# Encoder layer on one core: the last gate half turned through DRAM, attention parts of the output projection first, down groups ending on two plain units

## The chip, the cores and the metric

The kernel runs on one core of one Trainium2 chip. The metric is device time in microseconds (us) of one execution; lower is better. Of the kernel before, three runs gave a median of 1146.52 us (1145.9 to 1146.56).

## The reference

One layer of a bidirectional encoder for 256 tokens of 2048 features, all in fp32. With `norm` for RMS normalisation with a gain:

```
u = norm(x) @ w_in                       # 2048 -> 5120: q, k, v (1024 each), xr, yg (1024 each)
attn = neighbourhood_attention(q, k, v)  # 8 heads of 128, 4x64 grid of tokens
rec  = rglru_bidirectional(xr) * gelu(yg)        # conv, two gated scans; 8 blocks of 128
mixed = [norm(attn), norm(rec)] @ w_out  # 2048 -> 2048
h = x + norm(mixed)
f = norm(h)
ff = (silu(f @ w_gate) * (f @ w_up)) @ w_down    # 2048 -> 5632 -> 2048
h = h + norm(ff)
h = h + norm(sigmoid(norm(h) @ w_ple_gate) * (p @ w_ple_proj))
```

## The kernel before, in words

**Products.** Every fp32 operand is split into a rounded part `hi` and a remainder `lo`, and a product is the sum of three TensorE passes, hi x hi, hi x lo and lo x hi (lines 573 to 575, and 585 to 587 in pair units). A weight tile is 256 rows by 512 columns, [128, 2, 512] in SBUF. SP loads it (line 499), ScalarE casts it to `wh` (line 524), VectorE subtracts to get `wl` (line 534), TensorE uses it for both halves of 128 tokens. There are four raw and six split buffers, one more of each in the second half of the kernel, and more that are lent later.

**Order.** The input projection has ten chunks of 512 columns (the last two, `O_G` and `O_G + N`, are the gate `yg`), each of eight tiles. The output projection has, for each of four column ranges c, an attention part (blocks 0 to 7 of `mixT`) and a recurrent part (blocks 8 to 15), each of four tiles, in the order (0, attention), (1, attention), (0, recurrent), (1, recurrent), (2, a), (3, a), (2, r), (3, r). The two parts of one c are scaled by different token norms, so they are accumulated apart: `attn_part` puts the first into `mg` (line 1675), `rec_part` adds the second (line 1689); for c = 3 ScalarE writes the scaled attention part into the banks in which the recurrent part goes on (line 1707). Then come two small embedding chunks, and the FFN: eleven gate/up groups f0 to f10 of 512 columns, in parts of four, four and three, and after each part its down groups (two, two, and one with two single chunks). Each group takes its rows in units of 256 rows for two column ranges. A unit is plain ("p", two tiles, 2 x 12 = 24 passes of 512 columns) or a pair ("s", seven products instead of eight in Strassen's manner, 21 passes). For a pair VectorE makes two more tiles from differences of the two loaded ones (lines 554 and 558, two instructions each), which are cast and split like loaded ones. `KINDS` and `DOWN` list the units: three pairs in most groups.

**End of a group.** After the last pair `early` evacuates the banks `p1`, `p6`, `p5`, `p7` (lines 1761 to 1774); after the last unit `late` adds the four banks `c11` to `c22`. Groups take their two sets of four PSUM banks, rings `acc` and `sm`, in turn, so the next group's `c` banks are those that `early` frees. Down groups of parts 1 and 2 add onto the sums of the parts before: `seed_next` lets ScalarE copy these from `mg` into the `c` banks (line 625, `seed_group`) before TensorE goes on there. It is called ahead of the last unit of a group.

**Turning.** An output of the projection has tokens on partitions; what follows needs features on partitions. `turned` lets VectorE transpose 32x32 blocks (line 350), writes the tile to DRAM (`via`, line 356) and reads it back in four pieces with the partitions regrouped (line 364), for which the weight's columns are permuted on the host. Seven chunks of the input projection go this way. The values v need no turn, and the last gate half goes another way: `yg_post(1)` evacuates it with Gelu (line 892), TensorE transposes it in eight 128x128 pieces (line 340, in `transposed`), and VectorE multiplies from PSUM (line 1078 in `gate_pair`).

**Norm of the recurrent part.** `gate_pair` squares the gated blocks and adds them into `ssr` (lines 1066 and 1068). `token_rstd` sums over partitions by a TensorE product with a column of ones into `pb_rec` (line 1051), then root and reciprocal. After the second attention part `open_p2` waits until the planner has issued all splits of `mixT` and both norms, closes the first pool and opens the second in its place (with `mg`, the residual `h`, gains, one more buffer each); it also queues the loads of the gain, p and h.

**The planner.** The program order on each engine is written out by `Plan`, a list scheduler with costs for each engine: `act` 0.12 + 0.00082 n, `dve` 0.08 + 0.00104 n for n columns, `MM` 0.2267 us a pass, a DMA of kb at 340 KB/us; after a DMA of a turn it books `VIA` = 2.0 us. TensorE's order is fixed by the loops; other work becomes a generator that yields its next operation, and the one with the least start + lateness goes next. Casts of weights have the lateness

```
return LATE if at[0] - at_pe[0] >= 2 else -STARVE
```

that is LATE (0.6) while they are two tiles ahead of TensorE. Each engine runs its queue in that order, TensorE and SP too; what waits holds up all behind it.

Of the kernel before, what the change touches and what calls it, by code (L numbers as in the profile page):

```python
# [10 lines left out]
F32 = mybir.dt.float32  # L11
# [5 lines left out]
P = 128  # L17
S = 256
# [40 lines left out]
SM_BUFS = 4  # L59
LATE = 0.6  # L60
MM = 0.2267
# [3 lines left out]
TURN_LATE = -6.0  # L65
DOWN = (("p2 p6 s0 p8 p10 s4 s12 p14", "p2 p6 s0 p10 s4 p8 s12 p14"), ("p2 p6 s0 p8 p10 s4 s12 p14", "p2 p6 s0 p10 s4 p8 s12 p14"), ("p2 s0 p6 s4 p8 p10",))
URGENT = -2.0
# [16 lines left out]
LATE_SUMS = 0.0  # L84
SEED = 0.0
SAME_FROM = 320.0
SAME = ("dve", "act")
# [5 lines left out]
FIRST = "ppppspsp"  # L93
KINDS = tuple({"2": "ppppspsp", "3": "ppspspsp"}[f] for f in "32333333333")
ALL = ["s" if "s" in k else "p" for k in zip(*KINDS)]
# [164 lines left out]
def layer(ctx: ExitStack, tc: tile.TileContext, a: dict, out: bass.AP):  # L260
# [391 lines left out]
    def run_group(g, flip):  # L652
# [225 lines left out]

    def evac(ch, func, tables, turns=True):

        yield ev_x
        e = None
        for t in range(NT):
            yield act(N, tables, take="ev" if t == 0 else None)
            if e is None:
                e = t1["pool"].tile([P, 2 * N], F32, tag="ev", name="ev")
                if turns:
                    e = e.rearrange("p (c t n) -> p c t n", c=4, t=NT)
                else:
                    e = e.rearrange("p (t n) -> p t n", t=NT)  # L890
            to, src = (e[:, :, t, :], quarters(ch.accs[t])) if turns else (e[:, t, :], ch.accs[t])
            nc.scalar.activation(to, src, func, scale=rstd_x[:, t : t + 1])
        release(ch)
        if not turns:
            return e
        read = Event()
# [149 lines left out]
    def token_rstd(ss, n):  # L1046

        yield pe(0.44, take="sm")
        pb = bank(f"pb_{n}")
# [35 lines left out]
    def yg_post(hf):  # L1085
        def post(ch):
            b0 = hf * HB
            e = yield from evac(ch, AF.Gelu_apprx_tanh, GELU, not hf)
            yield ev_rec[hf + 1]
            if hf:  # L1090
                yield ev_rec[3]
            both = [Event() for _ in range(2)]
            if not hf:
                h4 = by_block(t1["hs"][:, b0 : b0 + HB, :])
                yield dve(4 * S)
                nc.vector.tensor_tensor(out=h4, in0=e, in1=h4, op=ALU.mult)
                plan.free["ev"].append(plan.now)
            for i in range(2):
                plan.add(gate_pair(b0, 2 * i, e if hf else None, both[i]), plan.now, SOON)
            for ev in both:  # L1100
# [609 lines left out]

    for c, rec in ((0, 0), (1, 0), (0, 1), (1, 1), (2, 0), (3, 0), (2, 1), (3, 1)):
        late = R_SEED if c == 3 else 0.0
        if c == 3:
            seg(r3 if rec else Chunk(a3_post, None, R_SEED), "w_out", c * N, mixT, R_KS if rec else A_KS)
        elif rec:
            seg(Chunk(rec_part(c), None, late, "acc" if c == 1 else "sm"), "w_out", c * N, mixT, R_KS)
        else:
            seg(Chunk(attn_part(c), open_p2 if c == 1 else None, late), "w_out", c * N, mixT, A_KS)
    embedding(0)
# [154 lines left out]
    for part, (f0, f1) in enumerate(parts):  # L1874
# [7 lines left out]
        for f in range(f0, f1):  # L1882
            Group(("w_ffn_gate", "w_ffn_up"), (f * N, f * N), hF,
                  [(k, k) for k in ORDER], KINDS[f % len(KINDS)] if f else FIRST, Gated(mid, (f - f0) * 4))
        last_lent[0] = len(tiles)
# [275 lines left out]
```

## Time and profile before

| what | value |
| --- | --- |
| median of three runs | 1146.52 us |
| the profiled execution's own time | 1148.39 us |
| its span, first to last instruction | 1146.6 us |
| mean granted TensorE clock | 0.996 of full speed |
| busy share of the span: TensorE, VectorE, ScalarE | 99%, 87%, 63% |
| HBM read, written | 242.04 MB, 14.68 MB |

The profiled execution is one run, 1.87 us over the median; its time is 1.79 us longer than its span. PE is TensorE, PEld its weight loads, DVE is VectorE, ACT is ScalarE, SP issues the DMAs (SPq is its sequencer). Passes of TensorE are pipelined: the start of one to the start of the next tells more than the busy time of one. Times in rows of a timeline count from the start of the span.

### The profile page before, as it was taken

How to read it: one execution, taken by the hardware profiler on the slowest of the kernel's cores; microseconds unless marked ns; L12 is line 12 of the kernel's file. 1: busy time of each engine (PE TensorE's matmuls, PEld its weight loads, DVE VectorE, ACT ScalarE, POOL GpSimd, SP SyncE). 2: the span in 40 equal slices, each digit the busy share in tenths (PEclk: the TensorE clock that was granted, in tenths of full speed). 3: DMA queues.
4: the chain of work that ended last, by engine and by line, in shares of the span. 5: the costliest groups of instructions: out<-in, count | busy, mean ns of one | idle time of the engine just before them, and what ended most of it. 6: DMA issues, size and time to landing. Idle time of an engine off the chain costs nothing.

```text
span 1146.6 us, 14712 instructions
## 1 busy us (share of the span) xinstructions
PE 1131.4 (99%) x5120; PEld 938.6 (82%) x5120; DVE 996.1 (87%) x1314; ACT 725.0 (63%) x986; POOL 1.6 (0%) x13
## 2 busy tenths in 40 slices
PE   9999999999999999999999999999999999999996
PEld 7888888888888888888888888888788888788885
DVE  6777888777659999999999998999998999987986
ACT  7775888697558754564555554565646546577864
POOL 0000000000000000000000000000000000000000
PEclk9999999999999999999999999999999999999998
DMA  9977868567866786685676766765667757885651
GB/s 355 290 237 197 258 189 248 166 184 263 314 194 229 225 256 217 205 260 198 218 242 203 216 220 185 239 236 196 235 199 236 217 184 213 313 321 191 195 173 73
DMA packets 83882, 257.69 MB, mean 225 GB/s; under 512 B 9056, under 2 KB 24800, under 8 KB 82656
## 3 DMA queue, kind: packets, MB, share of 16 engines
q1 hardware_dynamic: 83664, 256.68, 68.6%
q8 instruction: 40, 0.66, 0.2%
q14 instruction: 34, 0.28, 0.1%
q10 hardware_dynamic: 144, 0.08, 0.0%
HBM read 242.04 MB, written 14.68 MB: 224 GB/s over the span
## 4 chain that ended last, share of the span: by engine, by line
PE 83%; DVE 8%; DMA 3%; ACT 2%; issue 2%; SPq 1%; DVEq 0%; ACTq 0%
PE c L575 11%; PE c L573 11%; PE c L574 11%; PE acc L574 11%; PE acc L575 11%; PE acc L573 11%; PE p L586 3%; PE p L587 3%; PE p L585 3%; DVE wl L534 3%; PE c L586 2%; PE c L587 2%; PE c L585 2%; ACT wh L524 1%; DMA wr<-in_w_ffn_down 1%
## 5 line engine op out<-in xcount | busy, mean ns | idle before, releaser
L534 DVE TENSOR_TENSOR wl<-wr,wh 128x1024 fp32r<-128x1024 f32 (+1 forms) x321 | 364.6, 1163 | 64.2 <-ACT wh L524 63.5
L524 ACT CAST wh<-wr 128x1024 fp32r<-128x1024 f32 (+1 forms) x321 | 314.8, 1003 | 96.8 <-PE acc L575 43.5
L524 ACT CAST wh<-lent_t 128x1024 fp32r<-128x1024 f32 x78 | 81.8, 1053 | 163.1 <-DVE lent_t L558 148.7
L573 PE MATMUL c<-wh,hT_mix_hi 128*128 128x512 f32 x404 | 157.5, 390 | 0.0
L574 PE MATMUL c<-wl,hT_mix_hi 128*128 128x512 f32 x404 | 157.2, 389 | 0.0
L575 PE MATMUL c<-wh,hT_mix_lo 128*128 128x512 f32 x404 | 157.2, 389 | 0.0
L573 PE MATMUL acc<-wh,hT_hi 128*128 128x512 f32 x320 | 126.3, 395 | 1.3 <-ACT wh L524 1.3
L574 PE MATMUL acc<-wl,hT_hi 128*128 128x512 f32 x320 | 125.2, 391 | 0.2 <-DVE wl L534 0.2
L575 PE MATMUL acc<-wh,hT_lo 128*128 128x512 f32 x320 | 125.4, 392 | 0.0
L534 DVE TENSOR_TENSOR wl<-lent_t,wh 128x1024 fp32r<-128x1024 f32 x78 | 94.7, 1217 | 7.5 <-ACT wh L524 6.6
L573 PEld LDWEIGHTS c<-wh,hT_mix_hi 128*128 128x128 f32 x404 | 75.9, 188 | 16.0 <-ACT ple L1640 0.2
L574 PEld LDWEIGHTS c<-wl,hT_mix_hi 128*128 128x128 f32 x404 | 75.9, 188 | 15.7 <-DVE wl L534 0.2
L575 PEld LDWEIGHTS c<-wh,hT_mix_lo 128*128 128x128 f32 x404 | 75.8, 188 | 15.7
L573 PEld LDWEIGHTS acc<-wh,hT_hi 128*128 128x128 f32 x320 | 60.6, 189 | 13.4 <-ACT wh L524 1.5
L575 PEld LDWEIGHTS acc<-wh,hT_lo 128*128 128x128 f32 x320 | 60.4, 189 | 12.8
L574 PEld LDWEIGHTS acc<-wl,hT_hi 128*128 128x128 f32 x320 | 60.4, 189 | 12.5 <-DVE wl L534 0.5
L534 DVE TENSOR_TENSOR wl<-lent_r,wh 128x1024 fp32r<-128x1024 f32 (+1 forms) x58 | 64.8, 1135 | 1.5 <-ACT wh L524 1.5
L524 ACT CAST wh<-lent_r 128x1024 fp32r<-128x1024 f32 (+1 forms) x58 | 55.8, 982 | 10.0 <-PE c L575 5.0
L585 PE MATMUL p<-wh,sums_f 128*128 128x512 f32 x85 | 33.1, 389 | 0.0
L586 PE MATMUL p<-wl,sums_f 128*128 128x512 f32 x85 | 33.1, 389 | 0.0
L587 PE MATMUL p<-wh,sums_f 128*128 128x512 f32 x85 | 33.1, 389 | 0.0
L524 ACT CAST lent_w<-lent_t 128x1024 fp32r<-128x1024 f32 x12 | 12.6, 1052 | 25.1 <-DVE lent_t L558 25.1
(507 smaller groups left out, 2379.2 us busy)
## 6 DMA issues: line engine op xcount, KB each, us to landing
wr<-in_w_in SPq DMA_DIRECT2D x77, 512.0 KB, 4.8
wr<-in_w_ffn_down SPq DMA_DIRECT2D x70, 512.0 KB, 4.7
wr<-in_w_ffn_gate SPq DMA_DIRECT2D x64, 512.0 KB, 4.5
wr<-in_w_ffn_up SPq DMA_DIRECT2D x64, 512.0 KB, 4.2
wr<-in_w_out SPq DMA_DIRECT2D x32, 512.0 KB, 4.4
lent_r<-in_w_ffn_up SPq DMA_DIRECT2D x24, 512.0 KB, 4.0
lent_r<-in_w_ffn_gate SPq DMA_DIRECT2D x24, 512.0 KB, 4.5
wr<-in_w_ple_gate SPq DMA_DIRECT2D x24, 512.0 KB, 4.4
```

What stands on the lines that cost most here:

```text
L524: nc.scalar.copy(his[i][:, j, :], raws[i][:, j, :])
L534: nc.vector.tensor_tensor(out=los[i][:, j, :], in0=raws[i][:, j, :], in1=f32(his[i][:, j, :]), op=ALU.subtract,)
L573: nc.tensor.matmul(accs[t], hi[t], wh[:, j, :], start=st, stop=False, **mm)
L574: nc.tensor.matmul(accs[t], hi[t], wl[:, j, :], start=False, stop=False, **mm)
L575: nc.tensor.matmul(accs[t], lo[t], wh[:, j, :], start=False, stop=sp, **mm)
L585: nc.tensor.matmul(o, lh, wh, start=start, stop=False, **mm)
L586: nc.tensor.matmul(o, lh, wl, start=False, stop=False, **mm)
L587: nc.tensor.matmul(o, ll, wh, start=False, stop=stop, **mm)
```

## The change

- The last gate half is evacuated, turned and multiplied like the first; the columns `O_X + DR + N` of `w_in` are permuted on the host for it, and the path with TensorE's transposes goes.
- `token_rstd` for the recurrent norm waits 4.5 us of planned time before its ones product is queued.
- The output projection takes all four attention parts, then the four recurrent parts; the third and fourth attention parts accumulate in ring `sm`. The second pool opens after the third attention part, not the second.
- The seeds are asked for after the last pair of a group (`SEED_EARLY`), not ahead of its last unit. The call comes earlier only where a group has more than one plain unit behind its last pair.
- The unit orders of the down groups change: three of the four groups of parts 0 and 1 end on two plain units. The number of pairs in them stays.
- Gate group f7, the last of part 1, has two pairs, not three; the FFN has 44 pairs, not 45.
- `LATE` is 0.7, not 0.6.
- `EARLY` is empty, so `ORDER_2` and `KINDS_2` are not used.

```
-LATE = 0.6
+LATE = 0.7
-DOWN = (("p2 p6 s0 p8 p10 s4 s12 p14", "p2 p6 s0 p10 s4 p8 s12 p14"), ("p2 p6 s0 p8 p10 s4 s12 p14", "p2 p6 s0 p10 s4 p8 s12 p14"), ("p2 s0 p6 s4 p8 p10",))
+DOWN = (("p2 p6 s0 p8 s4 p10 s12 p14", "p2 p6 s0 p10 s4 s12 p8 p14"), ("p2 p6 s0 p8 s4 s12 p10 p14", "p2 p6 s0 p10 s4 s12 p8 p14"), ("p2 s0 p6 s4 p8 p10",))
+PARTS = ((0, 0), (1, 0), (2, 0), (3, 0), (0, 1), (1, 1), (2, 1), (3, 1))
+RINGS = {(0, 0): "acc", (1, 0): "acc", (2, 0): "sm", (3, 0): "sm", (0, 1): "acc", (1, 1): "acc", (2, 1): "acc"}
+OPEN = 2
+REC_WAIT = 4.5
+SEED_EARLY = True
-KINDS = tuple({"2": "ppppspsp", "3": "ppspspsp"}[f] for f in "32333333333")
+KINDS = tuple({"2": "ppppspsp", "3": "ppspspsp"}[f] for f in "32333332333")
...
                 if n == strassens[-1]:
                     plan.add(g.post.early(g), plan.clk["pe"] + plan.SEM, EARLY_EVAC)
+                    if SEED_EARLY:
+                        seed_next()
                     plan.run()
                 continue
-            if n == len(g.units) - 1:
+            if n == len(g.units) - 1 and not SEED_EARLY:
                 seed_next()
...
     def token_rstd(ss, n):
 
+        there = Event()
+        there.t = plan.now + (REC_WAIT if n == "rec" else 0.0)
+        yield there
         yield pe(0.44, take="sm")
...
-    def gate_pair(b0, b, e, ev):
+    def gate_pair(b0, b, ev):
         hs, sq = t1["hs"], t1["sqr", b // 2]
         h2 = hs[:, b0 + b : b0 + b + 2, :]
-        if e is not None:
-            tr = yield from transposed(e, b)
-            if b == 2:
-                plan.free["ev"].append(plan.now)
-            yield dve(2 * S, give="sm")
-            nc.vector.tensor_tensor(out=h2, in0=tr, in1=h2, op=ALU.mult)
...
-            e = yield from evac(ch, AF.Gelu_apprx_tanh, GELU, not hf)
+            e = yield from evac(ch, AF.Gelu_apprx_tanh, GELU)
...
-            if not hf:
-                h4 = by_block(t1["hs"][:, b0 : b0 + HB, :])
-                yield dve(4 * S)
-                nc.vector.tensor_tensor(out=h4, in0=e, in1=h4, op=ALU.mult)
-                plan.free["ev"].append(plan.now)
+            h4 = by_block(t1["hs"][:, b0 : b0 + HB, :])
+            yield dve(4 * S)
+            nc.vector.tensor_tensor(out=h4, in0=e, in1=h4, op=ALU.mult)
+            plan.free["ev"].append(plan.now)
...
-    for c, rec in ((0, 0), (1, 0), (0, 1), (1, 1), (2, 0), (3, 0), (2, 1), (3, 1)):
+    for c, rec in PARTS:
```

## Rows read from the trace of the kernel before

**Rows 1.** The page: busy us, share of the span and instructions of each engine.

```profile
PE 1131.4 (99%) x5120; PEld 938.6 (82%) x5120; DVE 996.1 (87%) x1314; ACT 725.0 (63%) x986; POOL 1.6 (0%) x13
```

**Rows 2.** Table by stage, output projection and first FFN groups: busy us, clock, DMA.

```profile
253.00:341.70 88.70, 88.70 (x399) 73.59 (x398) 60.99 (x72) 53.20 (x71) 0.00 (x0) 1.00 0.73 245
360.00:518.00 158.00, 158.00 (x698) 130.73 (x697) 151.12 (x188) 93.88 (x117) 0.00 (x0) 1.00 0.73 236
```

Each row gives the stretch, its length, and busy us (instructions) of PE, PEld, DVE, ACT and POOL, the granted clock, the DMA share and GB/s.

**Rows 3.** Waits of TensorE: who waited for whom, us, times, longest us.

```profile
PE c L573 <- ACT c L625: 1.8, 2, 1.6
...
PE p L586 <- DVE wl L534: 0.5, 1, 0.5
...
PE tr L340 <- DVE hT_mix_lo L328: 0.3, 1, 0.3
PE c L575 <- DVE mid2l L322: 0.3, 1, 0.3
```

**Rows 4.** Timeline of TensorE, part 1's down groups: start, length, operation, [idle before].

```profile
768.14 0.39 PE L575 MATMUL c<-wh,mid1l 128*128 128x512 f32 x1
768.70 0.50 PE L573 MATMUL c<-wh,mid1h 128*128 128x512 f32 x1 [0.17 <-ACT c L625]
...
810.09 0.39 PE L575 MATMUL c<-wh,mid1l 128*128 128x512 f32 x1
812.08 0.50 PE L573 MATMUL c<-wh,mid1h 128*128 128x512 f32 x1 [1.60 <-ACT c L625]
```

**Rows 5.** Timeline of VectorE ahead of the second of these waits.

```profile
804.73 4.62 DVE L534 TENSOR_TENSOR wl<-wr,wh 128x1024 fp32r<-128x1024 f32 x4
809.27 0.68 DVE L1764 TENSOR_TENSOR mid<-p,mid 128x512 f32<-128x512 f32 x1
```

**Rows 6.** Timeline of all engines, last pair of down group one.

```profile
801.31 1.23 DVE L534 TENSOR_TENSOR lent_w<-lent_t,lent_w 128x1024 fp32r<-128x1024 f32 x1 [1.17 <-ACT lent_w L524]
...
803.06 0.39 PE L586 MATMUL p<-lent_w,turned 128*128 128x512 f32 x1
...
804.19 0.39 PE L573 MATMUL c<-wh,mid1h 128*128 128x512 f32 x1
```

**Rows 7.** Timeline of TensorE, transposes of the last gate half.

```profile
259.88 0.39 PE L575 MATMUL acc<-wh,attn_lo 128*128 128x512 f32 x1
260.11 1.04 PE L340 MATMUL tr<-ident,ev 128*128 128x128 f32 x8
...
261.22 0.40 PE L574 MATMUL acc<-wl,attn_hi 128*128 128x512 f32 x1
```

**Rows 8.** Timeline of all engines, the turn of the first gate half.

```profile
235.58 1.25 DVE L350 STREAM_TRANSPOSE ev<-ev 128x1024 f32<-128x1024 f32 x1 [1.35 <-ACT ev L892]
...
236.86 0.33 SPq L356 DMA_DIRECT2D via<-ev  x1
...
239.91 1.84 SPq L364 DMA_DIRECT2D ev<-via  x4
```

**Rows 9.** VectorE's groups from 722 to 853: busy us, mean ns of one.

```profile
L534 DVE TENSOR_TENSOR wl<-lent_t,wh 128x1024 fp32r<-128x1024 f32 x16 | 19.5, 1219 | 1.4 <-ACT wh L524 1.2
...
L558 DVE TENSOR_TENSOR lent_t<-wr,lent_t 128x512 f32<-128x512 f32 x8 | 5.5, 692 | 0.3
```

**Rows 10.** Timeline of all engines where the second attention part ends.

```profile
276.46 0.39 PE L573 MATMUL acc<-wh,rec_hi 128*128 128x512 f32 x1
...
276.93 2.41 ACT L1675 ACTIVATE mg<-acc,r_attn 128x512 f32<-128x512 f32 x4
```

**Rows 11.** Page's DMA issues (us to landing), and landing of all that touch `via`.

```profile
ev<-via SPq DMA_DIRECT2D x28, 128.0 KB, 5.5
...
DMA to landing us min/median/max: 2.6/5.3/8.0
```

**Rows 12.** Timeline of all engines, the ones product of the recurrent norm.

```profile
265.33 0.89 DVE L1068 TENSOR_TENSOR ssr<-ssr,sqsqr 128x256 f32<-128x256 f32 x2
...
266.45 0.50 PE L1051 MATMUL pb_rec<-ones,ssr 128*128 128x1 f32 x4
```

More of the change, by code (lines that the diff above doesn't have):

```diff
@@ L85 @@
 SEED = 0.0
+PARTS = ((0, 0), (1, 0), (2, 0), (3, 0), (0, 1), (1, 1), (2, 1), (3, 1))
+RINGS = {(0, 0): "acc", (1, 0): "acc", (2, 0): "sm", (3, 0): "sm", (0, 1): "acc", (1, 1): "acc", (2, 1): "acc"}
+OPEN = 2
+REC_WAIT = 4.5
+EARLY = ()
+ORDER_2 = (0, 2, 4, 6, 8, 12, 10, 14)
+KINDS_2 = "ppspsspp"
+SEED_EARLY = True
 SAME_FROM = 320.0
@@ L877, in second_tiles, with evac @@
         mixT.blocks(t1["rec_hi"], t1["rec_lo"], 8, NB)
-    def evac(ch, func, tables, turns=True):
+    def evac(ch, func, tables):
         yield ev_x
@@ L885, in evac @@
             if e is None:
[L886 to L892, printed above, removed]
+                e = t1["pool"].tile([P, 4, NT, P], F32, tag="ev", name="ev")
+            nc.scalar.activation(
+                e[:, :, t, :], quarters(ch.accs[t]), func, scale=rstd_x[:, t : t + 1]
+            )
         release(ch)
-        if not turns:
-            return e
         read = Event()
@@ L1092, in post @@
             both = [Event() for _ in range(2)]
-            if not hf:
-                h4 = by_block(t1["hs"][:, b0 : b0 + HB, :])
-                yield dve(4 * S)
-                nc.vector.tensor_tensor(out=h4, in0=e, in1=h4, op=ALU.mult)
-                plan.free["ev"].append(plan.now)
+            h4 = by_block(t1["hs"][:, b0 : b0 + HB, :])
+            yield dve(4 * S)
+            nc.vector.tensor_tensor(out=h4, in0=e, in1=h4, op=ALU.mult)
+            plan.free["ev"].append(plan.now)
             for i in range(2):
-                plan.add(gate_pair(b0, 2 * i, e if hf else None, both[i]), plan.now, SOON)
+                plan.add(gate_pair(b0, 2 * i, both[i]), plan.now, SOON)
             for ev in both:
@@ L1709, in a3_post @@
         done(r3.seeded)
-    for c, rec in ((0, 0), (1, 0), (0, 1), (1, 1), (2, 0), (3, 0), (2, 1), (3, 1)):
+    for c, rec in PARTS:
         late = R_SEED if c == 3 else 0.0
         if c == 3:
-            seg(r3 if rec else Chunk(a3_post, None, R_SEED), "w_out", c * N, mixT, R_KS if rec else A_KS)
+            seg(r3 if rec else Chunk(a3_post, None, R_SEED, RINGS[3, 0]), "w_out", c * N, mixT, R_KS if rec else A_KS)
         elif rec:
-            seg(Chunk(rec_part(c), None, late, "acc" if c == 1 else "sm"), "w_out", c * N, mixT, R_KS)
+            seg(Chunk(rec_part(c), None, late, RINGS[c, rec]), "w_out", c * N, mixT, R_KS)
         else:
-            seg(Chunk(attn_part(c), open_p2 if c == 1 else None, late), "w_out", c * N, mixT, A_KS)
+            seg(Chunk(attn_part(c), open_p2 if c == OPEN else None, late, RINGS[c, rec]), "w_out", c * N, mixT, A_KS)
     embedding(0)
@@ L1883, in layer @@
             Group(("w_ffn_gate", "w_ffn_up"), (f * N, f * N), hF,
-                  [(k, k) for k in ORDER], KINDS[f % len(KINDS)] if f else FIRST, Gated(mid, (f - f0) * 4))
+                  [(k, k) for k in (ORDER_2 if f in EARLY else ORDER)],
+                  (KINDS_2 if f in EARLY else KINDS[f]) if f else FIRST, Gated(mid, (f - f0) * 4))
         last_lent[0] = len(tiles)
@@ L2139 @@
             w = w.copy()
-            for n0 in (O_X, O_X + N, 0, N, DA, DA + N, O_X + DR):
+            for n0 in (O_X, O_X + N, 0, N, DA, DA + N, O_X + DR, O_X + DR + N):
                 sl = slice(n0, n0 + N)
```

## Prediction

> **What bounds the kernel now.** I read the page's busy times first. TensorE is busy for 99% of the span [rows 1], so the only gains are TensorE work that vanishes and gaps in its queue; no other engine's saving counts by itself. The stage table gives the price of one product: in the first FFN groups 698 of them fill 158.00 us without a gap, 158.00 / 698 = 0.2264 us each [rows 2]. The same table has VectorE at 151.12 of these 158 us, so in the FFN it is the next bound, with 4% to spare; in the output projection it is at 60.99 of 88.70. Third, the list of waits of TensorE is short [rows 3]: besides the start, the largest is 1.8 us in two waits of a `c` product for ScalarE's copies of line 625, the seeds that put the running sum into the banks of the next down group. The others that matter here are 0.5, 0.3 and 0.3 us.
>
> TensorE's timeline shows where these two are [rows 4]. Products follow each other at 0.23 us; from 768.14 to the next is 0.56 us (0.33 lost), from 810.09 to the next 1.99 us (1.76 lost). Both lie three products into a down group of part 1, the first where the last gate group hands over to down group one, the second where that hands over to down group two. VectorE's timeline says why the second is long [rows 5]: when the last pair unit of down group one is over, 804.19 [rows 6], VectorE has four weight casts in its queue (4.62 us), and the evacuation that frees banks for seeds (line 1764) starts at 809.27. TensorE has only one plain unit meanwhile, 24 x 0.2264 = 5.43 us.
>
> **The change part by part.**
>
> *Gate half by VectorE and DRAM.* It removes eight TensorE transposes. They push the products at either side from 259.88 to 261.22, three steps that hold two products [rows 7]: 1.34 - 2 x 0.2264 = 0.89 us off the bound engine, -0.89. What it adds lies elsewhere: one VectorE transpose of 1.25 us, one multiply of a 1024-column tile that I bound by a cast of the same size (1.22 us, rows 9) less two smaller multiplies from PSUM, thus under 2.5 us on an engine with 27 us free in this stage; on SP's queue one write issue of 0.33 and four read issues of 1.84 us, and SP stands still until the write has landed: in the earlier half the write is issued at 236.86 and the reads at 239.91 [rows 8]. The output-projection loads queued behind these wait so long. TensorE waited for no such load in this stage, and the added 1 MB is 4.3 us at the stage's 245 GB/s, with a quarter of the DMA time idle [rows 2]. I take 0; the end above it stands at the ones product, below.
>
> The Trainium skill speaks against this part: "VectorE: DVE Perf Modes", section "Rules for kernel authors", advises TensorE for a 128x128 transpose whose result may lie in PSUM. By that rule the half is moved to the worse path, and the time would get longer by what the turn delays; that is the slower rival below. The rows agree that the turn takes far longer than 1.34 us, and differ on what counts, since TensorE is the full engine.
>
> *Attention parts first.* Before, the first product with recurrent blocks came at 276.46 [rows 10], after two attention parts. After four parts it comes 2 x 48 x 0.2264 = 21.7 us later, near 297 (with the transposes gone). The turned half must be split by then. The earlier half's chain: VectorE transpose until 236.83, reads issued from 239.91 [rows 8], the last about 1.4 us later, 5.5 us to landing [rows 11]: about 10 us. The last half's Gelu ended by 260.11, where TensorE transposes it [rows 7], so its data are back near 272, and multiply, squares and splits, some 8 us of VectorE and ScalarE work, end near 280, 17 us ahead of need. The second pool now opens after three parts, 10.9 us later, so the post gain, the residual and p tiles are loaded later and pass three more weight loads on SP; the mix norm reads them past 341. ScalarE evacuates six banks in a row instead of four (2.41 us, rows 10), 3.6 us, while the fourth part of 10.9 us runs from the other ring. 0.
>
> *Ones product later.* It stands in TensorE's in-order queue, and everything behind it waits if the sum of squares is late. Before, that sum ended at 266.13 and the product began at 266.45 [rows 12], so the plan had no spare time left. The plan books 7.0 us for a turn (2 x 512/340 + 2 x 2.0) against some 10.4 in the trace, 3.4 late; the added 4.5 us leave 4.5 + 0.3 - 3.4 = 1.4 us. A read of 8.0 us, the longest landing of any turn [rows 11], is 2.5 over the 5.5 used and would cost 1.1. Bounds 0 and 1.1; 0, as the median is the nearer row.
>
> *One pair fewer.* A pair unit has 21 products, a plain one 24: 3 x 0.2264 = +0.68 on TensorE, certain. VectorE loses two casts of sum tiles and four half-sums, 2 x 1.219 + 4 x 0.692 = 5.2 us [rows 9], in the eighth gate group, right ahead of the wait at 768. That wait was 0.33, and its seeds wait on VectorE: -0.33.
>
> *Down groups ending on two plain units, seeds after the last pair.* At the second handover the evacuation chain has 5.43 us more. Before, its seeds came 1.76 late; now they are 3.7 us early, and with two further casts put ahead of them (2 x 1.22) still 1.2 early: -1.76. The price is elsewhere: in down group one of part 1 the two back-to-back pairs lose the plain unit ahead of them. A pair costs VectorE 4 casts and 4 half-sums, 7.6 us in 4.75 us of TensorE; a plain unit 2 casts, 2.4 us in 5.43, so without it VectorE comes 3.0 us later to the pairs. It was ahead by 0.52 us at the tightest tile there (cast until 802.54, product at 803.06, rows 6). Nothing of the 5.2 us kept: 0.5 - 3.0 = 2.5 us of wait; half of it kept: none. In the first group of part 0 a pair comes one plain unit earlier too, with no relief ahead of it. Bounds 0 and 2.5; the nearest row is the one wait for a weight cast in a pair, 0.5 [rows 3]; with half of the relief likely kept I take +0.3.
>
> *The higher lateness* shifts evacuations ahead of casts by 0.1 us of planned time. Its price no row shows: bounds are the small waits of rows 3 going or doubling, 1.1 us listed; a listed 1.8 us lost 2.09 on the timeline, so 1.3 us either way; 0.
>
> Sum: -0.89 + 0.68 - 0.33 - 1.76 + 0.3 = -2.0 us. The profiled execution took 1148.39 us with a span of 1146.6; it would take 1146.4. It stands 1.87 over the median of 1146.52, and carried over the forecast is **1144.5 us**. If that 1.87 lay in the very waits that I remove, little would be left of the gain, 1146.3.
>
> **The rivals.**
>
> *The small waits go too.* If the new plan also clears the 0.5 (line 586), the 0.3 (line 575) and the 0.3 (line 340) and adds none: -2.30 - 1.3 = -3.6, 1142.9; with half of it 1143.6. For: all three wait on VectorE, and a higher lateness lets it finish splits earlier. Against: none lies close behind the relief of 5.2 us.
>
> *The pairs starve* in the first down groups: -2.30 + 2.5 = +0.2, 1146.7. For: a lead of 0.52. Against: the relief just ahead.
>
> *The change doesn't do it*: the planner puts all the new casts ahead of the evacuation, or seeds wait for something else, and 1.76 stays: 1146.3.
>
> *The turned half comes late* and TensorE stands at the ones product, the slower end. Each us beyond the 1.4 in hand is a us of the span; to be slower by over 0.2% it takes 2.3 + 2.3 = 4.6, a turn of over 16 us where 10.4 was seen, e.g. when SP holds it behind a load that has no buffer. With 5 us: 1149.2. Against: even the longest landing costs 1.1.
>
> **How the numbers follow.** A change of 0.2% (2.3 us, border 1144.2) is about what a measurement of this kernel can tell from none. My forecast has 0.46, with 1143.8 to 1145.4 of its own, so 0.16 of it under the border and 0.30 within; small waits going too 0.26, faster; starving pairs 0.15 and a wait that stays 0.05, both within; the late turn 0.08, slower. Faster 0.16 + 0.26 = 0.42, within 0.50, slower 0.08. The range runs from 1142.5 (all small waits gone, and 0.4 for the spread of the runs around their median) to 1147.2 (pairs starving with a 0.5 wait beside), and leaves out the late turn.
>
> **What would show it.** Right: no transposes of `ev` on TensorE; the wait for line 625 gone from its list; the ones product some 10 us later, behind products at 0.23 us steps; 3 products more, 8 transposes fewer. Wrong: a gap at the ones product; new waits for `wl` or `turned` near the consecutive pairs of the down groups; a wait for line 625 still over 1 us; or a time under 1143, which would mean that more than TensorE's visible gaps was to be had.

## The result and the profile after

Six runs of the changed kernel have a median of 1150.39 us (1148.11 to 1153.20), six of the kernel before beside them 1146.21 us (1144.22 to 1149.32). The ratio is 1.0038 with an interval of 1.0023 to 1.0054: slower by some 4 us, and outside the range forecast. The profiled execution took 1153.20 us with a span of 1151.4 and a mean granted clock of 0.995.

The page's busy times (before: [rows 1]) and TensorE's list of waits (before: [rows 3]), of the changed kernel (the line numbers are shifted: products are now 581 to 583, passes of pairs 593 to 595):

```profile
PE 1134.2 (99%) x5115; PEld 940.7 (82%) x5115; DVE 993.9 (86%) x1308; ACT 727.8 (63%) x984; POOL 1.6 (0%) x13
```
```profile
PE acc L581 <- ACT rt_rec L1064: 2.5, 1, 2.5
PE c L581 <- ACT mid2h L328: 1.6, 1, 1.6
...
PE c L583 <- DVE mid2l L330: 0.7, 1, 0.7
```

TensorE has five instructions fewer, as three more passes and eight transposes less must give. The wait for the seeds (`c` for ScalarE's copies) has left the list, and there is none for `wl` in a pair. Two new waits stand at its head. Where they cost, I read from the starts of TensorE's stages in both traces (after less before, so that a step in the difference is a gain or loss of the stage between):

| first product of | before | after less before |
| --- | --- | --- |
| parts 1, 2, 3, 4 of the output projection, in order (after: all attention parts) | 253.31, 265.08, 276.46, 287.34 | -0.34, -1.23, -1.73, -1.25 |
| part 5 in order (after: the first recurrent part) | 298.22 | +3.18 |
| gate group f7 | 726.21 | +3.17 |
| down groups one, two of part 1 | 767.69, 809.63 | +3.85, +3.38 |
| f8 | 853.01 | +1.49 |
| the last down group | 977.45 | +1.49 |
| the chunk behind it | 1010.07 | +4.62 |

So the fourth part in order lost 4.43 us and the last down group 3.13; everything between went as forecast (-0.89 at the transposes, +0.68 for the pair, -0.47 and -1.89 at the two handovers of part 1).

**The fourth attention part.** Timelines of VectorE, TensorE and ScalarE of the changed kernel:

```profile
281.64 0.43 DVE L1076 TENSOR_TENSOR ssr<-ssr,sqsqr 128x256 f32<-128x256 f32 x1
...
284.26 0.50 PE L1059 MATMUL pb_rec<-ones,ssr 128*128 128x1 f32 x4
...
286.56 0.40 PE L583 MATMUL acc<-wh,at_lo 128*128 128x512 f32 x1
289.50 0.80 PE L581 MATMUL acc<-wh,at_hi 128*128 128x512 f32 x1 [2.55 <-ACT rt_rec L1064]
...
286.83 1.05 ACT L532 CAST wh<-wr 128x1024 fp32r<-128x1024 f32 x1 [3.68 <-DMA wr<-in_w_out]
287.89 1.28 ACT L1064 ACT_TABLE_LOAD   x1
289.19 0.26 ACT L1064 ACTIVATE rt_rec<-pb_rec,eps 128x2 f32<-128x2 f32 x1
```

The ones product does not wait: its sum ended at 282.07, 2.2 us ahead (before, 0.3 us: [rows 12]). But parts three and four both accumulate in ring `sm`, of four banks. Part three holds two and `pb_rec` one. The first 128 tokens of part four find the last free bank, the second 128 wait for the bank of `pb_rec`. ScalarE frees it with its root (line 1064), and the root stands in ScalarE's queue behind a weight cast that waits 3.68 us for its tile from HBM, and behind a table load of 1.28 us.

**The last down group.** Timelines of SyncE, ScalarE and TensorE, first of the kernel before, then of the changed one:

```profile
973.21 0.90 SPq L1558 DMA_DIRECT2D h<-kept  x2
979.90 0.81 SPq L499 DMA_DIRECT2D wr<-in_w_ffn_down  x2
986.00 0.33 SPq L356 DMA_DIRECT2D via<-mid  x1
988.28 1.43 SPq L499 DMA_DIRECT2D wr<-in_w_ffn_down  x2
989.80 1.81 SPq L364 DMA_DIRECT2D turned<-via  x4
...
994.69 1.99 ACT L524 CAST wh<-wr 128x1024 fp32r<-128x1024 f32 x2
996.65 1.06 ACT L320 CAST mid2h<-turned 128x1024 fp32r<-128x1024 f32 x1
```
```profile
980.79 0.42 SPq L1559 DMA_DIRECT2D h<-kept  x1
986.04 0.33 SPq L364 DMA_DIRECT2D via<-mid  x1
986.41 0.43 SPq L1559 DMA_DIRECT2D h<-kept  x1
989.54 1.74 SPq L372 DMA_DIRECT2D turned<-via  x4
991.39 10.30 SPq L507 DMA_DIRECT2D wr<-in_w_ffn_down  x6
...
994.73 1.05 ACT L532 CAST wh<-wr 128x1024 fp32r<-128x1024 f32 x1
999.03 1.05 ACT L532 CAST wh<-wr 128x1024 fp32r<-128x1024 f32 x1 [3.25 <-DMA wr<-in_w_ffn_down]
999.98 1.04 ACT L328 CAST mid2h<-turned 128x1024 fp32r<-128x1024 f32 x1
...
999.11 0.39 PE L595 MATMUL c<-wh,mid2l 128*128 128x512 f32 x1
1001.08 0.50 PE L581 MATMUL c<-wh,mid2h 128*128 128x512 f32 x1 [1.58 <-ACT mid2h L328]
```

In both kernels ScalarE casts two weight tiles ahead of `mid2h`, the split of the turned last gate group, on which the last two plain units wait. Before, two tiles are asked for between the turn's write and its reads. After, the residual `h` (1 MB a piece) is reloaded on both sides of the write, the tiles follow the reads, and the second cast waits 3.25 us. `mid2h` comes 3.3 us later, 1.8 of them beyond the 1.49 by which the whole stage is late.

When the turn's own data were there, the view of `turned` tells (the four reads: first and last issue, then the times to landing), first of the kernel before, then of the changed one:

```profile
L364 SPq DMA_DIRECT2D turned<-via x4: 383/423/430, 989.8 to 991.2; - x4
DMA to landing us min/median/max: 4.9/5.1/5.3
```
```profile
L372 SPq DMA_DIRECT2D turned<-via x4: 319/430/432, 989.5 to 990.9; - x4
DMA to landing us min/median/max: 6.0/6.5/7.0
```

Before, the last read landed near 996.5 and `mid2h` began at 996.65. After, it landed near 997.9, and `mid2h` began at 999.98, 2.1 us later: the data were there, and ScalarE stood at the weight tile that had been asked for behind them.

**Half clock behind both.** The stage table of the changed kernel (stretch, length, busy us of each engine, granted clock, DMA share, GB/s):

```profile
286.50:289.50 3.00, 0.45 (x2) 0.02 (x2) 1.35 (x3) 2.64 (x4) 0.00 (x0) 0.99 0.85 318
289.50:292.80 3.30, 3.30 (x8) 2.62 (x9) 0.20 (x2) 3.30 (x7) 0.00 (x0) 0.50 0.93 343
...
1002.80:1006.20 3.40, 3.40 (x9) 2.64 (x9) 3.33 (x5) 2.98 (x6) 0.00 (x0) 0.50 0.73 245
```

After each of the two places TensorE has 1.2 GHz for 3.4 us, and its passes come every 0.43 us where 0.23 is usual: eight of them cost 1.6 us more. Of the 4.43 us of the fourth part, 2.7 are the wait (2.94 from start to start) and 1.6 this. In the last down group there are two waits (1.97 and 1.12 us from start to start, 2.6 lost) and this; two smaller ones of the trace before, together 1.1, are gone.

### The profile page after: what moved, and what is told of

It is laid out like the page before. It is cut to its first block, busy times and chain, and to the rows that moved or that the text cites. A ratio compares the mean times of both kernels' runs of the same rounds, so it can differ in the third digit from the quotient of the medians.

```text
span 1151.4 us, 14700 instructions
## 1 busy us (share of the span) xinstructions
PE 1134.2 (99%) x5115; PEld 940.7 (82%) x5115; DVE 993.9 (86%) x1308; ACT 727.8 (63%) x984; POOL 1.6 (0%) x13
## 4 chain that ended last, share of the span: by engine, by line
PE 85%; DVE 6%; DMA 4%; ACT 3%; issue 2%; SPq 0%; DVEq 0%; ACTq 0%
PE c L583 12%; PE c L581 12%; PE c L582 12%; PE acc L581 10%; PE acc L582 10%; PE acc L583 10%; PE p L594 3%; PE p L595 3%; PE p L593 3%; PE c L595 2%; PE c L593 2%; PE c L594 2%; DVE wl L542 2%; DMA wr<-in_w_out 1%; ACT wh L532 1%
## 5 line engine op out<-in xcount | busy, mean ns | idle before, releaser
L532 ACT CAST wh<-wr 128x1024 fp32r<-128x1024 f32 (+1 forms) x322 | 318.3, 1008 | 131.3 <-PE acc L583 41.4
L581 PE MATMUL c<-wh,hT_mix_hi 128*128 128x512 f32 x416 | 162.2, 390 | 0.0
L583 PE MATMUL c<-wh,hT_mix_lo 128*128 128x512 f32 x416 | 161.9, 389 | 0.0
L582 PE MATMUL c<-wl,hT_mix_hi 128*128 128x512 f32 x416 | 161.8, 389 | 0.0
L532 ACT CAST wh<-lent_t 128x1024 fp32r<-128x1024 f32 x75 | 78.5, 1053 | 111.3 <-DVE lent_t L566 88.9
L542 DVE TENSOR_TENSOR wl<-lent_t,wh 128x1024 fp32r<-128x1024 f32 x75 | 91.0, 1217 | 10.4 <-ACT wh L532 9.7
L1832 ACT ACTIVATE mid<-mid,rstd_f 128x512 f32<-128x512 f32 x22 | 14.7, 717 | 37.1 <-DVE mid L1825 37.1
L593 PE MATMUL p<-wh,sums_f 128*128 128x512 f32 x81 | 31.5, 389 | 0.0
L595 PE MATMUL p<-wh,sums_f 128*128 128x512 f32 x81 | 31.5, 389 | 0.0
```

Of the source, the lines that this page charges most:

```text
L532: nc.scalar.copy(his[i][:, j, :], raws[i][:, j, :])
L542: nc.vector.tensor_tensor(out=los[i][:, j, :], in0=raws[i][:, j, :], in1=f32(his[i][:, j, :]), op=ALU.subtract,)
L581: nc.tensor.matmul(accs[t], hi[t], wh[:, j, :], start=st, stop=False, **mm)
L582: nc.tensor.matmul(accs[t], hi[t], wl[:, j, :], start=False, stop=False, **mm)
L583: nc.tensor.matmul(accs[t], lo[t], wh[:, j, :], start=False, stop=sp, **mm)
L593: nc.tensor.matmul(o, lh, wh, start=start, stop=False, **mm)
```

## The experiments

My theory was that both waits are real and add up. The first rival: all of it lies in one of them; others came up on the way. Before in the table is the kernel before, run beside each batch (17 to 35 runs); "d-last" is the length of the last down group in the profiled execution, less the 32.62 us of before in its first profile.

| run | median us | before | ratio and interval | d-last |
| --- | --- | --- | --- | --- |
| e1 bank given back by VectorE | 1150.32 | 1146.28 | 1.0028 (1.0012 to 1.0044) | +0.20 |
| e2 h reloaded later | 1149.40 | 1146.28 | 1.0024 (1.0010 to 1.0039) | +1.17 |
| e3 both | 1149.37 | 1146.28 | 1.0021 (1.0008 to 1.0035) | +1.88 |
| e4 FFN part alone | 1150.16 | 1146.28 | 1.0030 (1.0010 to 1.0050) | +2.63 |
| e5 down order and seeds alone | 1146.68 | 1145.98 | 0.9999 (0.9986 to 1.0013) | -0.78 |
| e6 44 pairs alone | 1148.70 | 1145.98 | 1.0027 (1.0008 to 1.0046) | +0.42 |
| e7 input side alone | 1148.00 | 1145.98 | 1.0012 (0.9993 to 1.0030) | -0.86 |
| e8 changed, 45 pairs, bank by VectorE | 1147.34 | 1145.98 | 1.0010 (0.9995 to 1.0025) | -0.16 |
| e10 input side, ones product earlier | 1144.70 | 1146.43 | 0.9984 (0.9973 to 0.9996) | -1.34 |
| e11 changed, 45 pairs, ones product earlier | 1144.64 | 1146.43 | 0.9984 (0.9972 to 0.9996) | -1.34 |
| e12 44 pairs alone, turn through POOL's queue | 1152.33 | 1146.43 | 1.0048 (1.0030 to 1.0066) | +4.84 |
| e13 43 pairs alone | 1147.07 | 1146.24 | 1.0006 (0.9991 to 1.0021) | -0.87 |
| e14 44 pairs alone, reads planned later | 1153.40 | 1146.24 | 1.0059 (1.0042 to 1.0076) | +6.89 |
| e15 44 pairs alone, pair taken from f10 | 1145.51 | 1146.24 | 0.9987 (0.9971 to 1.0004) | -0.85 |
| e16 changed, ones product earlier | 1146.90 | 1146.24 | 1.0007 (0.9989 to 1.0024) | +1.56 |
| e17 changed, pair from f10, ones product earlier | 1144.00 | 1145.84 | 0.9986 (0.9976 to 0.9996) | -1.33 |

e9 (before again) and e18 (changed again) are one execution each: 1145.92 and 1151.26 us, d-last -0.72 and +3.16.

**e1 to e3: take each wait away in the changed kernel.** e1 copies the column out of PSUM by VectorE; e2 plans the reload of `h` 10 us later; e3 does both.

```
+        src = pb[:, :, 0]
+        if n == "rec":
+            yield dve(NT, give="sm")
+            nc.vector.tensor_copy(out=tmp, in_=src)
+            src = tmp
+        yield act(NT, SQRT, give=None if n == "rec" else "sm")
+        nc.scalar.activation(tmp, src, AF.Sqrt, bias=eps, scale=1.0 / DA)
...
         yield ev_back["wr"]
+        later = Event()
+        later.t = plan.now + 10.0
+        yield later
         h_tiles()
```

> The changed kernel, but VectorE copies the two columns of pb_rec into SBUF and so gives its bank back; ScalarE's root reads the copy. Theory (bank): in the changed kernel the fourth attention part cannot open its second bank because pb_rec holds it, and its release, the root on ScalarE, stands behind a weight cast that waits for a load; the wait costs 2.7 us and the low clock after it 1.7 us. Then the wait of TensorE for rt_rec is gone, the clock stays high through 280 to 300, and the time is about 4.4 us below the changed kernel's (1146 where that has 1150.4). Rival (weights late): the stage is short of loaded weights, and TensorE will wait at the same place for a cast: at most 1.5 us gained. Rival (clock by itself): the low stretch stays though the wait goes: 2.7 us gained.

> The changed kernel, with the reload of the residual h asked for 10 us later, so that the two 1 MB loads stand behind the turn of the last gate group in SP's queue as they stood well ahead of it before the change. Theory (queue): in the last down group TensorE waits 1.6 and 0.7 us for mid2 because those loads share the DMA engines with the turn and with the weight load that stands ahead of the mid2 cast on ScalarE; with them behind the turn the waits fall to the 0.3 us or so of the kernel before, the low clock of 3.4 us behind them goes, and the time is some 3 us below the changed kernel's. Rival (VectorE): the mid2 split is late because VectorE is full there whatever the loads do: no change within 0.5 us.

> Both edits. If the two losses are independent their gains add: about 7.5 us below the changed kernel, 1143 where the kernel before has 1146.2, which is what the blind sum had (-2.0) and a bit more. If one of them only moves the wait on (the later stages start earlier and collide again) the sum falls short by 2 us or more.

None came back to the time of before, and all three forecasts missed. The edits did not remove the waits at the bank: in e1 and e3 the copy stands in VectorE's queue behind weight casts that wait for the same late tiles (2.08 and 2.53 us from start to start at the fourth part), and in e2, where it was left alone, this wait lost 0.9. In e2 two tiles stand between the turn's write and its reads again; `mid2h` waited 1.3 us for the reads instead of the weights, and TensorE still lost 1.2 us there (steps of 0.71 and 0.92). So they say nothing against the theory, but neither remedy is one.

**e4: only the FFN part of the change (new `DOWN`, early seeds, 44 pairs), on the kernel before.**

> The kernel before with the FFN part of the change alone (new unit orders, 44 pairs, seeds after the last pair; lateness, gate half and part order as before). Theory: the FFN part takes away 2.1 us of waits at the two seeded handovers, costs 0.7 us for the pair, and brings the reload of h next to the turn (its order on SP is that of the changed kernel), so some 3 us are lost in the last down group: 1 to 2 us slower than before. Rival: the late mid2 comes from the input side of the change (everything shifted, higher lateness): then 1.4 us faster than before.

1150.16 us: slower by 0.3% with the input side untouched, 3.9 us where 1 to 2 were expected. Its ten executions differ by 9.6 us, and the length goes with the clock: the four with a mean granted clock of 0.992 to 0.995 have spans of 1151.8 us in the mean, the three with 0.997 or 0.998 1144.4, as long as the 31 executions of before, whose clock is 0.996 to 0.998. So the loss differs from execution to execution, and a single profile can understate or overstate it.

**e5 and e6: which edit of the FFN part.** e5 has `DOWN` and the seeds and keeps 45 pairs; e6 is this line alone:

```
-KINDS = tuple({"2": "ppppspsp", "3": "ppspspsp"}[f] for f in "32333333333")
+KINDS = tuple({"2": "ppppspsp", "3": "ppspspsp"}[f] for f in "32333332333")
```

> The kernel before with the new order of the down groups and the seeds asked for early, but with its 45 pairs. Theory: in the FFN part the loss comes from the pair that was dropped, since without it SyncE's queue takes the reload of h on both sides of the turn's write instead of ahead of three weight tiles, and the last down group waits. With 45 pairs the queue is as before, so only the two seed waits go: -0.3 and -1.8 us, about 1144.2 us, mean granted clock 0.997 to 0.998 in every run as before. Rival A: the new order of the down groups or the early seeds themselves cost it: 1149 to 1150 us and a clock that varies from 0.992 to 0.998, as in the run of the whole FFN part.

> The kernel before with 44 pairs and nothing else. Theory: +0.7 us for the pair, and 2 to 4 us in the last down group (ScalarE's cast of mid2h stands behind a weight tile that was asked for late, then a stretch at half clock in some executions): 1149 to 1151 us, clock 0.994 to 0.998. Rival A (order of the down groups or seeds): +0.7 us alone, 1147.0 us, clock 0.997.

e6 is slower by 0.27%, a little less than expected, and e5 is as long as before: the dropped pair costs it, not the order or the seeds. But e5 missed its number too: the gain of 2.1 us at the seeds isn't there. Its median stood 0.7 us over before, and its interval excludes -0.18%.

**e7 and e8: the input side.** e7 is the changed kernel with the FFN part of before; e8 is the changed kernel with 45 pairs and e1's copy.

> The changed kernel with the FFN part of before (old down order, 45 pairs, late seeds). Theory: -0.9 us for the transposes, +2.4 us or so for the fourth attention part that waits for a bank of ScalarE's root at 286 us, and 1.7 us of half clock behind it in some executions: 1146.5 to 1149.5 us, clock 0.995 to 0.998. Rival B: the bank wait of the one profile is rare and the input side is a plain gain: 1145.4 us, clock as before.

> The changed kernel with 45 pairs again, and the bank of the ones product given back by a VectorE copy. Theory: the gains of the transposes (-0.9) and of the two seed waits (-2.1) stay, the wait for the bank is what it was with the copy (1.8 us and no half clock) or less: 1144 to 1146 us, and the first version below or at the time of before. Rival A: as with the copy alone, 1150 us. Rival C: half clock comes wherever a wait of over a microsecond does, so the bank wait alone still makes 1148 us.

TensorE's timeline in e7, at the second half of the fourth part:

```profile
285.74 0.40 PE L583 MATMUL acc<-wh,at_lo 128*128 128x512 f32 x1
287.27 0.50 PE L581 MATMUL acc<-wh,at_hi 128*128 128x512 f32 x1 [1.14 <-ACT rt_rec L1064]
```

The wait is there without any change to the FFN, and the time is where the theory put it, if with an interval that reaches below 1. e8 missed its 1146 us; its profile has a wait of 2.52 us (from start to start) for the copy and 3.4 us at half clock behind it, which is near rival C. As a rule rival C doesn't hold: no half clock followed the 1.53 us of e7.

**e9: the kernel before, profiled again**, for the missing gain of e5.

> The kernel before, unchanged, profiled once more. Theory: the seed waits at 768 us (0.3 us lost) and 810 us (1.8 us lost) that the prediction counted as gains belong to that one execution; this profile has neither, as the run with 44 pairs alone and the run of the input side alone have neither, though both ask for their seeds late. Rival: the waits stand in every execution of the kernel before, and the wait of 1.99 us from product to product near 810 us is here again.

```profile
809.54 0.39 PE L575 MATMUL c<-wh,mid1l 128*128 128x512 f32 x1
810.32 0.50 PE L573 MATMUL c<-wh,mid1h 128*128 128x512 f32 x1 [0.39 <-ACT c L625]
```

Near 768 us nothing is lost now, and near 810 us 0.55 where it was 1.76 [rows 4]. e6 and e7, which ask for seeds as late as the kernel before, have neither wait in their lists. The gain was real in the one trace and is not in the median.

**e10 and e11: remove the bank wait by order.** The ones product is queued 2.0 us later instead of 4.5; the root then stands ahead of the cast that waits.

```
-REC_WAIT = 4.5
+REC_WAIT = 2
```

> The input side alone, with the ones product 2.0 instead of 4.5 us later (24 products nearer to its place of before by half: 12 products), so that on ScalarE's queue the root stands ahead of the fourth weight cast, the one that waited 3.7 us for its tile. Theory (the bank held through ScalarE's queue is the loss of the input side): TensorE waits at most 0.7 us at the ones product and nothing at the fourth attention part; 1145.0 to 1145.8 us against 1148.0 with the wait, clock back at 0.997 to 0.998. Rival B: the time does not hang on this bank, 1147.5 to 1148.5 us again.

> The changed kernel with 45 pairs and with the ones product 2.0 us later. Theory: both losses are gone, what stays is the transposes' -0.9 us and perhaps the seed waits: 1143.5 to 1145.5 us, below the kernel before. Rival A (the new down order or the early seeds cost something where the profile does not show it): 1146.5 to 1147.5 us.

Timelines of TensorE and ScalarE in e10:

```profile
281.25 0.51 PE L1059 MATMUL pb_rec<-ones,ssr 128*128 128x1 f32 x4
...
283.08 0.26 ACT L1064 ACTIVATE rt_rec<-pb_rec,eps 128x2 f32<-128x2 f32 x1
...
285.50 1.05 ACT L532 CAST wh<-wr 128x1024 fp32r<-128x1024 f32 x1 [2.15 <-DMA wr<-in_w_out]
```

The bank is free at 283.3, ahead of the fourth part, and TensorE waits at neither place. The input side alone goes from 1.0012 to 0.9984; e10 lies 0.3 us under its forecast, e11 within it. That settles the first loss: the late tile is still late (2.15 us), and TensorE does not wait for it. Six profiles with the old place (the changed kernel, e1, e2, e3, e7, e8) and e18 have a gap of 1.17 to 2.94 us there; the four with the new one (e10, e11, e16, e17) have none.

**e12 to e15: how one pair costs 2 us, 250 us later.** SyncE's order of issues is that of the changed kernel, shown above, in all six profiles that drop f7's pair alone and leave that queue as it is planned (the changed kernel, e1, e4, e6, e16, e18). e12 is e6 with the write and the reads of the last turn sent through POOL's queue; e14 is e6 with the reads planned later, so that two tiles stand ahead of them; e13 drops two pairs (f6 and f7), e15 one, in f10. These two bring the reloads of `h` ahead of the write again, and two or three tiles between the write and the reads. The edits in this order (the line of `KINDS` that e12 and e14 share with e6 is left out):

```
-        nc.sync.dma_start(via, e.rearrange("p c t n -> p c (t n)"))
+        q = nc.gpsimd if own_queue[0] else nc.sync
+        q.dma_start(via, e.rearrange("p c t n -> p c (t n)"))
...
-            nc.sync.dma_start(
+            q.dma_start(
...
+            own_queue[0] = self.mid.blocks_of == 12 and self.kk0 == 8
...
-        out.t = plan.now + VIA
+        out.t = plan.now + (VIA if plan.now < 960.0 else 4.0)
...
-KINDS = tuple({"2": "ppppspsp", "3": "ppspspsp"}[f] for f in "32333333333")
+KINDS = tuple({"2": "ppppspsp", "3": "ppspspsp"}[f] for f in "32333322333")
...
-KINDS = tuple({"2": "ppppspsp", "3": "ppspspsp"}[f] for f in "32333333333")
+KINDS = tuple({"2": "ppppspsp", "3": "ppspspsp"}[f] for f in "32333333332")
```

> The kernel before with 44 pairs, where the write and the reads of the last gate group's turn go through POOL's queue, so that the weight tiles of the last down group no longer stand behind them on SyncE's. Theory (SyncE's order is what the dropped pair costs): 0.7 us for the pair and nothing in the last down group, 1146.5 to 1147.2 us, clock 0.997 to 0.998. Rival D: the last down group waits for the turn itself, whatever queue it runs through, and the time stays at 1148 to 1149 us with a clock from 0.994 on.

> The kernel before with two pairs dropped, one in f6 and one in f7. SyncE's queue then reloads h ahead of the last turn's write again, with three weight tiles behind each reload and three between the write and the reads. Theory (the order of that queue is the cost): +1.4 us for the two pairs and no more, 1147.4 to 1148.2 us with a clock of 0.997 to 0.998 in nearly all runs, and the last down group as long as in the kernel before or shorter. Rival E (each dropped pair costs more than its 0.68 us): 1149.5 to 1152 us.

> 44 pairs alone, with the reads of the last turn planned 2 us later, so that on SyncE's queue two weight tiles stand ahead of them as in the kernel before; the reloads of h stay around the turn's write. Theory (the two weight casts that stand ahead of the cast of mid2h wait for those tiles): 1147.0 to 1147.6 us, clock 0.997 to 0.998. Rival F (the reloads of h in the queue, or the turn itself, are what is late): 1148.5 to 1150 us as with 44 pairs alone.

> The kernel before with 44 pairs, where the dropped pair is one of f10, the last gate group, and not of f7. SyncE's queue then has both reloads of h ahead of the last turn's write and two weight tiles between write and reads. Theory (the queue's order): +0.7 us, 1147.0 to 1147.6 us, clock 0.997 to 0.998. Rival E (the number of pairs): 1148.5 to 1150 us and a clock that varies.

e13 and e15 speak for the queue's order and against the number of pairs: with 43 the time is 0.8 us over before, no more than two pairs cost (1.4), and with 44 from another group it is not above before at all. e13 is 0.3 us below its forecast, e15 1.5; why is open. Dropping a pair in f10 also takes VectorE work away right ahead of the last down group, which e13 does not. SyncE's and ScalarE's timelines in e15:

```profile
976.27 0.80 SPq L1558 DMA_DIRECT2D h<-kept  x2
981.97 0.32 SPq L356 DMA_DIRECT2D via<-mid  x1
983.11 1.43 SPq L499 DMA_DIRECT2D wr<-in_w_ffn_down  x2
984.92 2.15 SPq L364 DMA_DIRECT2D turned<-via  x4
...
994.90 1.05 ACT L320 CAST mid2h<-turned 128x1024 fp32r<-128x1024 f32 x1 [1.71 <-DMA turned<-via]
```

Here `mid2h` waits for its own data and for no weights. e12 missed: through POOL the reads were issued 5.25 us after the write (986.05, 991.30) where SyncE took 3.02 in e6 (984.50, 987.52), `mid2h` waited 3.4 us for them, and so it shows only that the turn has no slack there. e14 missed by more, since the planner put not two but five weight casts between the lent tiles and `mid2h`. ScalarE's timeline in e14:

```profile
993.84 1.05 ACT L524 CAST wh<-wr 128x1024 fp32r<-128x1024 f32 x1 [1.11 <-DMA wr<-in_w_ffn_down]
997.48 1.04 ACT L524 CAST wh<-wr 128x1024 fp32r<-128x1024 f32 x1 [2.60 <-DMA wr<-in_w_ffn_down]
998.76 1.04 ACT L524 CAST wh<-wr 128x1024 fp32r<-128x1024 f32 x1 [0.24 <-DMA wr<-in_w_ffn_down]
999.72 1.04 ACT L320 CAST mid2h<-turned 128x1024 fp32r<-128x1024 f32 x1
```

Its last read was issued at 987.0 and took 9.3 us, so the data were there at 996.3; `mid2h` began at 999.72, and TensorE stood 6.36 us from start to start. So 3.4 us of the delay are ScalarE's queue with casts that wait for tiles, and the rest is reads that took 9.3 us where they took 5.1 before. Neither edit put two tiles in that place and changed nothing else.

What e12 and e14 were to separate, the traces of the other kernels do. From the landing of the turn's last read to the start of `mid2h` it takes 2.1 or 2.2 us in all six profiles with the order of the changed kernel (in e6 from 993.8 to 995.8), and 0.1 or 0.2 us in the twelve that have two or three tiles between the write and the reads (the kernel before, e2, e3, e5, e7 to e11, e13, e15, e17). The late landing of the reads is no rival for this: in e6 they took 4.6 us, less than before, with `h` reloaded beside them. So a weight tile that is asked for behind the reads and cast ahead of `mid2h` holds it up by 2 us in each of these six; how much TensorE loses by it differs (in e6 it stopped only 0.7 us, for `mid2l`).

**e16 to e18: do the two losses add up?** e16 is the changed kernel with `REC_WAIT = 2.0`, e17 takes the pair from f10 besides, e18 is the changed kernel again.

> The changed kernel (44 pairs) with the ones product 2.0 instead of 4.5 us later, nothing else. Theory (two losses that add up): against the version with 45 pairs and this place (1144.6 us) it has the pair's 0.7 us and the 2 us of the last down group, 1147.0 to 1148.2 us; against the changed kernel it is 2 to 3 us faster. Rival: only one of the two losses is at work in most executions, so it stays at 1149 to 1150.5 us.

> The changed kernel with the ones product 2.0 us later and with the dropped pair taken from f10 in place of f7. Theory (two losses, both gone, with the pair in f10 worth what the run with it alone showed): 1143.7 to 1145.2 us, below the kernel before by 0.1 to 0.25%, clock 0.997 to 0.998. Rival: the pair in f10 gains nothing on top of the ones product's place, 1145.3 to 1146.5 us.

> The changed kernel unchanged, profiled once more. Theory: both waits are its own and not of one execution. TensorE stands 2 to 3.5 us ahead of the fourth attention part near 286 us, behind ScalarE's root, and 1.5 to 4 us in the last down group near 999 us, behind the cast of mid2h or of its low part; whether half clock follows differs. Rival: one of them is missing, as the wait of 1.99 us near 810 us was in the second profile of the kernel before.

From TensorE's list of waits, e18's, then what is left in e17's beside the start and small ones:

```profile
PE c L581 <- ACT mid2h L328: 2.2, 1, 2.2
PE acc L581 <- ACT rt_rec L1064: 1.4, 1, 1.4
...
PE c L583 <- DVE mid2l L330: 0.4, 1, 0.4
```
```profile
PE acc L582 <- DVE wl L542: 0.5, 2, 0.2
PE tr L348 <- DVE hT_mix_lo L336: 0.3, 1, 0.3
```

Both waits are the changed kernel's own. The losses add: from the changed kernel (1.0038) to e16 (1.0007) the bank is worth 0.31%, 3.6 us; from e16 to e11 (0.9984) the pair of f7 is worth 0.23%, 2.6 us, 0.7 of it its three passes. What is left is the gain, 0.16%, 1.8 us. e10, without any edit to the FFN, has the same 0.9984, so the order of the down groups, the early seeds and the lateness together gain nothing that shows in a median. The transposes are 0.89 of the 1.8; the rest is within the interval, and e10's and e11's last down group, which has no wait left, is 0.6 us shorter than in e9 and 1.3 than in the first profile of before. Each difference has the uncertainty of two intervals, about 0.2%. e17, the change with two corrections of one constant each, beats both kernels: 1144.00 us, 0.9986 with an interval of 0.9976 to 0.9996. e16 lies 0.1 us under its forecast, e17 within it.

## Why the prediction was wrong

- *Gate half by VectorE and DRAM*: right. -0.89 forecast, -0.89 between the first two parts in the traces of the changed kernel, e7, e10 and e11. The data were back at 274.38 (the multiply's start), for 272 forecast. The Trainium skill ("VectorE: DVE Perf Modes", section "Rules for kernel authors") advises TensorE for a 128x128 transpose whose result may lie in PSUM, and the late turn that the prediction feared from going against it did not come: the sum was ready 2.2 us ahead of its product, and with the bank free the input side gains 0.16%.
- *Attention parts first*: here it failed. The step said "while the fourth part of 10.9 us runs from the other ring. 0." The fourth part runs from the same ring as the third, and I counted no banks: three parts in flight hold six, `pb_rec` a seventh, and the fourth part needs two of eight. In place of the 0 the runs put 3.6 us on it, and the first trace 4.43.
- *Ones product later*: its bounds, 0 and 1.1, asked whether TensorE would wait at the product. It didn't. What the step lacked is that the product's result holds a bank until ScalarE has come to the root, and ScalarE's queue had a cast ahead that waits for HBM. The product also came 17.8 us later than before (284.26 against 266.45), not "some 10 us", and so its bank was still held when part four began.
- *One pair fewer*: the +0.68 was measured as 0.68. Taking it for the whole price was the second failure: 1.9 us more came with it, by the last down group, through an order of queues that shifts with the tiles that a pair takes or leaves. No rival named it.
- *The seed waits*: -0.33 and -1.76 were measured as -0.47 and -1.89 against that one trace, and as nothing in e5's median. The prediction had said that the profiled execution's 1.87 us over the median might lie in these very waits; e9 is 2.47 us shorter than that execution and has 1.54 us less of these waits, so this was most of it; the case deserved more than a sentence.
- *Starving pairs*, +0.3: no such wait in the changed kernel's trace; a single one of 1.01 us from start to start in e5's, and one of 1.21 in e10's, which has the old order. The step priced only the first down groups; in the second ones, too, two pairs now follow each other, and the changed kernel's trace has no such wait there either. *Lateness*, 0: not tried alone.
- The rivals: the time went to the slower side, but not by the late turn, which was the only one there. A range built on terms that were all read from TensorE's own gaps had no room for waits that the trace of before does not have.

## What to carry to other kernels

When parts of a contraction are reordered, count the banks that are held at each moment, the small results included, and for each ask in whose in-order queue its last reader stands and what waits ahead of it there. Before pricing a unit less or more, lay the issue order of the DMA queue of both builds side by side for the whole kernel: a shift by one tile can undo an order that a much later stage lives on. Where an operand comes late, compare the landing of its data with the start of its first reader: what lies between is the queue, not the DMA. And take a wait as a gain only if a second profile of the same kernel has it.

## What the runs showed of the hardware

A single stop of TensorE can be followed by 3.41 us at 1.2 GHz: in the changed kernel after 2.94 us from start to start, in e3 and e8 after 2.53 and 2.52, in e14 after 6.36 us (6.8 us at this clock, some of it in the stop). It did not follow the 1.99 us of the kernel before, nor the 2.08 us in e1 and the 1.81 us in e18's fourth part, while in e4 it came after two stops of 1.44 and 1.12 us close together. In e16, two stops of 1.38 and 1.12 us at the same place had no such stretch behind them. So nearly the same wait is 1.6 us dearer in one execution than in another. In e4 the length of the ten executions goes with their mean clock, so this is part of the 9.6 us between them; as only one or two executions of a kernel were profiled, how large a part is not shown.

The time that the four reads of the last turn take to land, all of one size, differs much between executions: medians of 4.6 us in e6, 5.1 in the kernel before, 6.5 in the changed one, 7.2 in e18, 8.2 in e15 and 9.3 in e14. The reload of `h` alone does not decide it: it runs beside the reads in e6 (4.6) and is over before them in e8 and e17 (6.9 and 6.8). What decides it is not shown.
